# First loads, transposes and roundings in turns by K tile, squares later, constant products ahead of them, and operands at multiples of 512 bytes

## The chip, the core and the metric

The kernel runs on one core of a Trainium2 chip. A core has TensorE (PE), VectorE (DVE), ScalarE (ACT), GpSimd (POOL) and SyncE (SP, which here only issues DMAs). Each works through its own queue in order. The time is the device time of one execution in microseconds (us); lower is better.

## The reference

Two decoder layers over x, 256 tokens by 2048 features, float32:

```python
for l in range(DEPTH):                      # DEPTH = 2
    h = rmsnorm(x, attn_norm_g[l])
    q, k, v, gate_b, gate_c, conv_in = split(h @ w_in[l])      # 2048 x 6144
    attn = diff_attention(rmsnorm(q), rmsnorm(k), v, lam, rel_bias)   # 8 heads
    conv = gate_b * short_conv(gate_c * conv_in, conv_w[l])    # causal, 3 taps
    x = x + concat([rmsnorm(attn) * (1 - lam_init), conv]) @ w_out[l]
    x = x + relu(rmsnorm(x) @ w_up[l]) ** 2 @ w_down[l]        # 2048 x 8192 x 2048
```

All weights are float32 and are read once; the products with them are most of the work.

## The kernel before

Precision is kept by splitting every operand of a product into a rounded part (`hi`, type float32r) and the rest (`lo`). A product is then three TensorE instructions for each K tile of 128 rows: hi x hi, hi x lo, lo x hi (`TERMS`). The rounding is a copy on ACT (line 282 for weights, `whi`; line 248 for activations, `nT`), the rest a subtraction on DVE (line 283, `wlo`; line 249).

`linear` (line 325) makes 256 tokens by 512 columns out of 16 K tiles. Its weights come in jobs of two K tiles (512 KB, tile `raw`, four buffers). `Weights.take` hands out a job's halves and makes the halves of jobs up to three ahead (`AHEAD`). With `cut`, the first two jobs of the program are rounded one K tile at a time. After each K tile `linear` calls `work.tick()`: this advances the side work, a list of generators that each say after how many ticks they go on. So PE's order (which is the program's order) has transposes, norms and attention put between the products at fixed ticks. The order on the other engines is made by a planner, which takes its own estimate of when an operand is ready; `late` pins an instruction behind the one traced before it on its engine.

At the start of the program:

- x comes in four blocks of 512 columns, `load_x` (line 133). Block 0 is issued first, in two halves, then two weight jobs, block 1, two weight jobs, blocks 2 and 3, all on SP's queue.
- The norm's gains (`ngv`) are loaded from ACT's queue, transposed on PE (`gps`, line 152) and copied to `ngains`.
- `Norm.chunk(n)` transposes block n on PE (line 402, `tpn`, eight transposes into two PSUM banks), multiplies by the gains while it rounds (`split_gained`, lines 248 and 249), and at once takes the squares for the norm (line 412, `junk`). Block 0 goes first, the others at ticks of the first product.
- `Norm.factors` waits until all four blocks are transposed and makes the row scales; the norm itself is applied to the product's result, not to its operand. A broadcast of the scales (`rbc`, line 444) goes through PE.
- `qk_norm` (yield at line 474) normalises q and k after their products and transposes them eight ticks later.

The constants lie in a pool of their own at the lowest addresses (tiles are rounded up to 32 bytes per partition); pools of large tiles follow, and SBUF is full but for 160 bytes per partition.

Of the kernel before, what the change touches and what calls it, by code (L numbers as in the profile page):

```python
# [9 lines left out]
F32 = mybir.dt.float32  # L10
F32R = mybir.dt.float32r
AF = mybir.ActivationFunctionType
# [3 lines left out]
P = 128  # L16
DEPTH = 2
D = 2048
S = 256
NT = S // P  # L20
AW = 1024
NH = 8
# [6 lines left out]
CH = 512  # L29
WC = 256  # L30
KG = 4
RAW = 4
AHEAD = 3
# [68 lines left out]
def trunk(ctx: ExitStack, tc: tile.TileContext, x, w_in, w_out, conv_w, q_norm_g, k_norm_g,  # L102
          lambda_q1, lambda_k1, lambda_q2, lambda_k2, subln_g, attn_norm_g, mlp_norm_g,
          w_up, w_down, rel_bias, selector, out):
    nc = tc.nc
    PSUM = bass.MemoryType.PSUM
    const = ctx.enter_context(tc.tile_pool(name="const", bufs=1))
# [6 lines left out]
    mm = ctx.enter_context(tc.tile_pool(name="mm", bufs=2, space=PSUM))  # L114
    ps = ctx.enter_context(tc.tile_pool(name="ps", bufs=3, space=PSUM))
    ctx.enter_context(tc.manual_schedule(engines={mybir.EngineType.PE}))

    def late(ins):

        tc.keep_in_program_order(ins)  # L120

    def bank(name):
        return ps.tile([P, CH], F32, tag="bank", name=name)

    def wide(name):
        return nat.tile([P, CH], F32, tag="wide", name=name)

    work = Background()


    xs = [xpool.tile([P, NT, CH], F32, tag=f"x{n}", name=f"x{n}") for n in range(D // CH)]

    def load_x(n, cuts=1):
        for c in range(cuts):
            lo, hi = c * CH // cuts, (c + 1) * CH // cuts
            nc.sync.dma_start(
                xs[n][:, :, lo:hi],
                x[0, :, n * CH + lo:n * CH + hi].rearrange("(t p) c -> p t c", p=P))

    NG = DEPTH * D // P  # L140
    ngv = const.tile([NG, P], F32, tag="ngv", name="ngv")
    nc.scalar.dma_start(ngv, attn_norm_g.rearrange("l (k p) -> (l k) p", p=P))
    load_x(0, 2)

    ident = const.tile([P, P], F32, tag="ident", name="ident")
    make_identity(nc, ident)
    mhalf = const.tile([P, NH], F32, tag="mhalf", name="mhalf")
    nc.vector.memset(mhalf, -0.5)


    gps = bank("gps")
# [4 lines left out]
    def norm_gain(which, l, k):  # L156
        i = l * (D // P) + k
        return gains[:, MG + i:MG + i + 1] if which else ngains[:, i:i + 1]
# [19 lines left out]
    rel = const.tile([NB + 1, 2 * NH], F32, tag="rel", name="rel")  # L178
    nc.vector.memset(rel[NB:NB + 1, :], NEG)
    nc.gpsimd.dma_start(rel[0:NB, :], rel_bias)  # L180
    ones = const.tile([P, P], F32, tag="ones", name="ones")
    nc.vector.memset(ones, 1.0)

    gains = const.tile([P, ROWS], F32, tag="gains", name="gains")
    q_gain = const.tile([P, DEPTH], F32, tag="qg", name="q_gain")
    k_gain = gains[:, QG + DEPTH:QG + 2 * DEPTH]
# [59 lines left out]
    def split_gained(dst, k, src, gain):  # L246

        nc.scalar.activation(dst[:, 0, k], src, AF.Copy, scale=gain)  # L248
        nc.vector.scalar_tensor_tensor(
            dst[:, 1, k], src, gain, dst[:, 0, k].bitcast(F32), op0=ALU.mult, op1=ALU.subtract)  # L250
# [14 lines left out]
    class Weights:  # L265
# [5 lines left out]
            self.jobs, self.made, self.used = [], [], 0  # L271
            self.early = []

        def halves(self, raw, c=slice(None)):

            i = len(self.made)
            shape = [P] + list(raw.shape[1:])
            hi = wpool.tile(shape, F32R, tag="hi", name="whi")
            lo = wpool.tile(shape, F32R, tag="lo", name="wlo")
            first = self.cut and i < 2  # L280
            for k in (slice(0, 1), slice(1, None)) if first else (slice(None),):
                nc.scalar.activation(hi[:, k], raw[:, k], AF.Copy)  # L282
                nc.vector.tensor_sub(lo[:, k], raw[:, k], hi[:, k].bitcast(F32))  # L283
            return hi, lo

        cut = False

        def plain(self, w, row, c, nk):

            cols = 2 * CH // nk  # L290

            def make():
                raw = self.early.pop(0) if self.early else load()
                return self.halves(raw)

            def load():
                raw = self.pool.tile([P, nk, cols], F32, tag="raw", name="raw", bufs=RAW)
                nc.sync.dma_start(
                    raw, w[row:row + nk * P, c:c + cols].rearrange("(k p) c -> p k c", p=P))
                return raw  # L300

            make.load = load
            self.jobs.append(make)

        def load_early(self, n):

            for _ in range(n):
                self.early.append(self.jobs[len(self.early)].load())

        def take(self):  # L310
            i = self.used
            self.used += 1
            while len(self.made) < min(len(self.jobs), i + 1 + AHEAD):
                self.made.append(self.jobs[len(self.made)]())
            return self.made[i]

# [68 lines left out]
    class Norm:  # L385
# [2 lines left out]

        def __init__(self, which, l):
            self.which, self.l = which, l  # L390
            self.tiles = [Parts(apool, "a", f"nT{which}{l}_{n}") for n in range(D // CH)]
            self.ss = small.tile([P, NT, D // CH], F32, tag="ss", name=f"ss{which}{l}", bufs=2)

        def chunk(self, n, wait):
            yield wait
            a = self.tiles[n].open()
            for j in range(2):
                tp = bank(f"tpn{n}_{j}")
                for i in range(2):
                    k = 2 * j + i  # L400
                    for t in range(NT):
                        nc.tensor.transpose(  # L402
                            tp[:, i * S + t * P:i * S + (t + 1) * P],
                            xs[n][:, t, k * P:(k + 1) * P], ident)
                for i in range(2):
                    k = 2 * j + i
                    split_gained(a, k, tp[:, i * S:(i + 1) * S],
                                 norm_gain(self.which, self.l, n * KG + k))
            self.tiles[n].ready = True
            for t in range(NT):  # L410
                junk = wide(f"junk{n}_{t}")
                sq = nc.scalar.activation(junk, xs[n][:, t], AF.Square,
                                          accum_out=self.ss[:, t, n:n + 1])
                if (self.which, self.l) == (0, 0):
                    late(sq)

        def factors(self):
            while not all(t.ready for t in self.tiles):
                yield 1
            tot = small.tile([P, NT], F32, tag="tot", name="tot")  # L420
            nc.vector.tensor_reduce(tot, self.ss, axis=AX.X, op=ALU.add)
            r = rstd_of(tot, D, "row", NT)
            self.r = small.tile([P, NT], F32, tag="rowf", name="rowf", bufs=2)
            nc.vector.tensor_copy(self.r, r)
            diag = small.tile([P, NT, P], F32, tag="diag", name="diag", bufs=1)
            if self.which:

                self.scale = small.tile([P, 1], F32, tag="rowf2", name="rowf2")
                nc.vector.tensor_mul(self.scale, r[:, 1:2], r[:, 1:2])
                ratio = small.tile([P, 1], F32, tag="ratio", name="ratio")  # L430
                nc.vector.reciprocal(ratio, r[:, 1:2])
                nc.vector.tensor_mul(ratio, ratio, r[:, 0:1])
                nc.vector.tensor_scalar_mul(diag[:, 0], ident, ratio)
                yield 5
                tp = bank("rbc")
                nc.tensor.matmul(tp[:, :P], ones, diag[:, 0], start=True, stop=True)
                self.ratio = small.tile([P, P], F32, tag="rowb", name="ratiob", bufs=1)
                nc.vector.tensor_copy(self.ratio, tp[:, :P])
                return
            for t in range(NT):  # L440
                nc.vector.tensor_scalar_mul(diag[:, t], ident, self.r[:, t:t + 1])
            yield 5
            tp = bank("rbc")
            nc.tensor.matmul(tp[:, :S], ones, diag.rearrange("p t c -> p (t c)"),
                             start=True, stop=True)
            self.across = small.tile([P, 2, S], F32, tag="rowb", name="rowb", bufs=1)
            nc.vector.tensor_copy(self.across[:, 0], tp[:, :S])
            nc.gpsimd.tensor_tensor(self.across[:, 1], self.across[:, 0], self.across[:, 0],
                                    op=ALU.mult)
# [5 lines left out]
    def qk_norm(acc, r, dst, gain, name):  # L455

        out_ = []
        for t in range(NT):
# [6 lines left out]
            f = rstd_of(ms, DK, f"{name}{t}", NH)  # L465
# [5 lines left out]
                acc[:, t].rearrange("p (g d) -> p g d", d=DK),  # L471
                f2.unsqueeze(2).to_broadcast([P, NH, DK]), op=ALU.mult)
            out_.append(qn)
        yield 8
        for t in range(NT):
            tp = bank(f"{name}tp{t}")
            for i in range(4):
# [121 lines left out]
    def mixer(l, norm, loads):  # L599

        with ExitStack() as scope:
# [2 lines left out]
            rpool = scope.enter_context(tc.tile_pool(name="rpool", bufs=RAW))  # L604
            bpool = scope.enter_context(tc.tile_pool(name="bpool", bufs=8))
            weights = Weights(rpool)
            weights.cut = l == 0
            for half in range(2):
                for part in range(3):
                    weights.straight(w_in[l], 0, D // P, part * AW + half * CH)  # L610
# [373 lines left out]
    norm = Norm(0, 0)  # L984

    def first_loads(weights):
        for n in range(1, D // CH):
            weights.load_early(2)
            load_x(n)
            work.start(norm.chunk(n, 2), 4 * n - 3)  # L990

    work.start(norm.chunk(0, 0))
    for l in range(DEPTH):
        mnorm = mixer(l, norm, first_loads if l == 0 else lambda weights: None)
        norm = mlp(l, mnorm, l == DEPTH - 1)
# [31 lines left out]
```

## Time and profile before

| | |
|---|---|
| median of 3 runs | 2181.64 us (2178.86 to 2182.95) |
| the profiled execution | 2181.14 us |
| its span, first to last instruction | 2179.4 us |
| PE busy | 2156.6 us, 99% |
| DVE, ACT, POOL busy | 74%, 58%, 6% |
| DMA engines | 205 GB/s in the mean |

In the rows below a line of a group reads: line, engine, operation, out<-in, shape, xcount | busy us, mean ns of one | idle time before them and what ended it. A row of the timeline or of the chain begins with its start and its length in us. A row of a DMA issue ends with KB of one and the us from issue to landing. A row of a window gives its length, then each engine's busy us, the granted clock, the share of the DMA engines and GB/s.

### The profile page before, as it was taken

What the parts mean: (1) busy time and instruction counts of PE and PEld (TensorE: products, weight loads), DVE (VectorE), ACT (ScalarE), POOL (GpSimd) and SP (SyncE); (2) the same over time, 40 slices, a digit from 0 to 9 for tenths busy, and PEclk for the clock granted to TensorE, in tenths of its full rate; (3) what the DMA queues carried; (4) which work ended last, traced back from release to release, by engine and by line L of the source; (5) the groups of instructions that cost most, each with busy time, mean ns of one, the idle gap of its engine ahead of it and who ended that gap; (6) DMA issues with size and microseconds to landing.
All of it is one profiled execution on the core that took longest, in us unless ns stands there. A gap on an engine that the chain in (4) does not pass through costs nothing.

```text
span 2179.4 us, 29050 instructions
## 1 busy us (share of the span) xinstructions
PE 2156.6 (99%) x11066; PEld 1828.6 (84%) x11066; DVE 1603.9 (74%) x2229; ACT 1271.7 (58%) x1718; POOL 138.8 (6%) x194
## 2 busy tenths in 40 slices
PE   8999999999999999999999999999999999999999
PEld 6888888888888888888888888888888888888887
DVE  6677655698888888855566776557988888887554
ACT  6456445566666666654454654455666666665443
POOL 2021100000000000100011111000000000001000
PEclk9999999999999999999999999999999999999999
DMA  7555656476666666587565466656766666666774
GB/s 256 180 156 177 218 185 184 157 238 223 213 212 215 220 208 214 189 277 241 175 205 181 156 199 197 184 173 190 225 218 217 213 212 216 219 208 212 246 242 145
DMA packets 292491, 446.62 MB, mean 205 GB/s; under 512 B 10403, under 2 KB 191221, under 8 KB 292352
## 3 DMA queue, kind: packets, MB, share of 16 engines
q1 hardware_dynamic: 285648, 423.66, 61.5%
q0 software_dynamic: 6656, 21.10, 2.6%
q8 instruction: 86, 1.41, 0.3%
q14 instruction: 53, 0.43, 0.1%
q10 hardware_dynamic: 48, 0.02, 0.0%
HBM read 425.84 MB, written 18.90 MB: 204 GB/s over the span
## 4 chain that ended last, share of the span: by engine, by line
PE 94%; DMA 2%; DVE 2%; ACT 1%; issue 1%; SPq 0%; DVEq 0%; ACTq 0%
PE upc L809 29%; PE dn L969 15%; PE pr L849 13%; PE o L338 8%; PE q L338 4%; PE gc L360 4%; PE ci L360 4%; PE k L338 4%; PE gb L360 4%; PE v L338 4%; PE upw L809 1%; DMA uraw<-in_w_up_dram 1%; PE sc L500 1%; PE av L536 1%; PE tpn L402 1%; DMA draw<-in_w_down_dram 1%
## 5 line engine op out<-in xcount | busy, mean ns | idle before, releaser
L283 DVE TENSOR_TENSOR wlo<-raw,whi 128x1024 fp32r<-128x1024 f32 (+1 forms) x386 | 473.3, 1228 | 385.5 <-ACT whi L282 381.0
L282 ACT ACTIVATE whi<-raw 128x1024 fp32r<-128x1024 f32 (+1 forms) x386 | 406.8, 1055 | 477.8 <-PE dn L969 166.7
L809 PE MATMUL upc<-nT,uhi 128*128 128x512 f32 x1920 | 477.5, 391 | 0.0
L694 ACT ACTIVATE uhi<-uraw 128x1024 fp32r<-128x1024 f32 x256 | 271.2, 1060 | 287.3 <-PE upc L809 253.9
L809 PEld LDWEIGHTS upc<-nT,uhi 128*128 128x128 f32 x1920 | 352.7, 188 | 68.2
L695 DVE TENSOR_TENSOR ulo<-uraw,uhi 128x1024 fp32r<-128x1024 f32 x256 | 312.8, 1222 | 115.3 <-ACT uhi L694 112.9
L969 PE MATMUL dn<-whi,g 128*128 128x512 f32 x1024 | 316.4, 389 | 0.0
L809 PEld LDWEIGHTS upc<-nT,ulo 128*128 128x128 f32 x1920 | 261.9, 190 | 18.7
L809 PE MATMUL upc<-nT,ulo 128*128 128x256 f32 x1920 | 267.7, 282 | 0.0
L969 PEld LDWEIGHTS dn<-whi,g 128*128 128x128 f32 x1024 | 192.2, 188 | 39.7
L969 PE MATMUL dn<-wlo,g 128*128 128x512 f32 x512 | 199.6, 390 | 1.1 <-DVE wlo L283 1.0
L338 PE MATMUL o<-whi,cat 128*128 128x512 f32 x512 | 159.6, 390 | 0.0
L969 PEld LDWEIGHTS dn<-wlo,g 128*128 128x128 f32 x512 | 96.1, 188 | 22.6 <-DVE wlo L283 2.8
L338 PEld LDWEIGHTS o<-whi,cat 128*128 128x128 f32 x512 | 96.2, 188 | 19.7
L338 PE MATMUL o<-wlo,cat 128*128 128x512 f32 x256 | 99.6, 389 | 0.0
L831 POOL DMA_DIRECT2D hid<-h x64 | 34.9, 545 | 949.1 <-ACT h L830 913.4
L849 PE MATMUL pr<-t13h,f 128*128 128x512 f32 x240 | 93.8, 391 | 0.0
L338 PE MATMUL q<-whi,nT 128*128 128x512 f32 x256 | 86.4, 406 | 4.1 <-ACT nT L248 4.1
L338 PE MATMUL k<-whi,nT 128*128 128x512 f32 x256 | 85.3, 399 | 0.0
L849 PE MATMUL pr<-t24h,f 128*128 128x512 f32 x240 | 84.0, 391 | 0.0
L849 PE MATMUL pr<-b2h,f 128*128 128x512 f32 x240 | 84.0, 391 | 0.0
L338 PE MATMUL v<-whi,nT 128*128 128x512 f32 x256 | 83.4, 396 | 0.0
(330 smaller groups left out, 3431.0 us busy)
## 6 DMA issues: line engine op xcount, KB each, us to landing
uraw<-in_w_up_dram SPq DMA_DIRECT2D x128, 1024.0 KB, 5.9
raw<-in_w_in_dram SPq DMA_DIRECT2D x192, 512.0 KB, 3.9
draw<-in_w_down_dram SPq DMA_DIRECT2D x64, 1024.0 KB, 5.1
raw<-in_w_down_dram SPq DMA_DIRECT2D x64, 1024.0 KB, 5.7
raw<-in_w_out_dram SPq DMA_DIRECT2D x64, 512.0 KB, 3.6
hid<-h POOLq DMA_DIRECT2D x64, 256.0 KB, 4.3
back<-hid SPq DMA_DIRECT2D x32, 512.0 KB, 3.3
rev<-by_dist_d POOLq DMA_DIRECT2D x4, 1024.0 KB, 11.1
```

Source lines behind the costliest of these rows:

```text
L282: nc.scalar.activation(hi[:, k], raw[:, k], AF.Copy)
L283: nc.vector.tensor_sub(lo[:, k], raw[:, k], hi[:, k].bitcast(F32))
L338: nc.tensor.matmul(acc[:, t], a.ap[:, pa, k % KG, t * P:(t + 1) * P], (hi, lo)[pw][:, j], start=(k == 0 and n == 0), stop=(k == nk - 1 and ...
L360: nc.tensor.matmul(acc[:, f, 0] if part else acc[:, f], wt[:, k % 4, fs], a.ap[:, 0, k % KG] if part else a.ap[:, :, k % KG], start=(part ...
L402: nc.tensor.transpose(tp[:, i * S + t * P:i * S + (t + 1) * P], xs[n][:, t, k * P:(k + 1) * P], ident)
L500: nc.tensor.matmul(sc[:, :W], qT[m * DK:(m + 1) * DK, a, i, t * P:(t + 1) * P], kT[m * DK:(m + 1) * DK, b, i, :W], start=(n == 0), stop=(n ...
L694: nc.scalar.activation(hi, src, AF.Copy)
L695: nc.vector.tensor_sub(lo, src, hi.bitcast(F32))
L809: nc.tensor.matmul(acc[:, 0] if part else acc, wt[:, k], a.ap[:, 0, k % KG] if part else a.ap[:, :, k % KG], start=(part == 0 and kh == 0 ...
L831: nc.gpsimd.dma_start(hid[i // 2][:, i % 2 * 2 * S:(i % 2 + 1) * 2 * S], u)
L849: nc.tensor.matmul(prods[n], fs[j][:, pa, a], b[pw], start=(j == 0 and m == 0), stop=(stop and m == 2))
L969: nc.tensor.matmul(acc[:, t], f[:, pa, k, t * P:(t + 1) * P], (hi, lo)[pw][:, k % 2], start=(b == 0 and k == 0 and m == 0), stop=(b == NB2 ...
```

## The change

Five things change.

1. The first block of x and the first weight job are loaded in turns: half of the x block, the first K tile of weights, the other half, the second K tile. The other early loads keep their order.
2. `Norm.begin` transposes, rounds and splits block 0 one K tile at a time, and behind each K tile it rounds and splits the weights of that K tile (`part`). The instructions are pinned in this order.
3. The squares of blocks 0 to 2 come later: block 0's after all four K tiles, those of blocks 1 and 2 some ten ticks after their transposes. `factors` waits for the squares. The weights are made one job ahead at first, up to three ahead from the seventh job on (`ramp`).
4. `warm_up(n)` issues n products of a constant tile of ones (float32, 128 x 128 x 128) into a PSUM tile that nothing reads: 11 ahead of the first transpose, 3 after the second and 3 after the fourth K tile.
5. A tile `fill` of 128 bytes and a tile `started` are added to the constants, and `ngv` leaves them, so that the pools behind begin at a multiple of 512 bytes; they began 352 bytes past one.

`qk_norm` transposes 12 ticks later instead of 8.

```diff
+    const.tile([P, 32], F32, tag="fill", name="fill")
...
-    def load_x(n, cuts=1):
-        for c in range(cuts):
-            lo, hi = c * CH // cuts, (c + 1) * CH // cuts
-            nc.sync.dma_start(
+    def load_x(n, lo=0, hi=CH):
+        nc.sync.dma_start(
...
-    ngv = const.tile([NG, P], F32, tag="ngv", name="ngv")
+    ngv = wide("ngv")[:NG, :P]
     nc.scalar.dma_start(ngv, attn_norm_g.rearrange("l (k p) -> (l k) p", p=P))
-    load_x(0, 2)
+    ones = const.tile([P, P], F32, tag="ones", name="ones")
+    nc.vector.memset(ones, 1.0)
+    mhalf = const.tile([P, NH], F32, tag="mhalf", name="mhalf")
+    nc.vector.memset(mhalf, -0.5)
+    started = const.tile([P, 1], F32, tag="started", name="started")
+    nc.scalar.activation(started, mhalf[:, 0:1], AF.Copy)
+    warm = mm.tile([P, NT, CH], F32, tag="mm2", name="warm")
+
+    def warm_up(n):
+        for _ in range(n):
+            nc.tensor.matmul(warm[:, 0, :P], ones, ones, start=True, stop=True)
     ident = const.tile([P, P], F32, tag="ident", name="ident")
     make_identity(nc, ident)
+    warm_up(11)
...
         def halves(self, raw):
...
+            if not self.by_tile:
+                pair = (nc.scalar.activation(hi, raw, AF.Copy),
+                        nc.vector.tensor_sub(lo, raw, hi.bitcast(F32)))
+                if self.ramp and len(self.made) < 12:
+                    for ins in pair:
+                        late(ins)
             return hi, lo
...
+        def begin(self):
+            self.by_tile = self.ramp = True
+            raw = self.pool.tile([P, 2, CH], F32, tag="raw", name="raw", bufs=RAW)
+            w, row, c = self.first
+            for k in range(2):
+                load_x(0, k * CH // 2, (k + 1) * CH // 2)
+                nc.sync.dma_start(raw[:, k], w[row + k * P:row + (k + 1) * P, c:c + CH])
+            self.early.append(raw)
+            self.load_early(1)
+            raws = list(self.early)
+            self.made += [self.jobs[i]() for i in range(2)]
+            self.by_tile = False
+
+            def part(k):
+                (hi, lo), raw, j = self.made[k // 2], raws[k // 2], k % 2
+                late(nc.scalar.activation(hi[:, j], raw[:, j], AF.Copy))
+                late(nc.vector.tensor_sub(lo[:, j], raw[:, j], hi[:, j].bitcast(F32)))
+            return part
...
-            while len(self.made) < min(len(self.jobs), i + 1 + AHEAD):
+            ahead = min(AHEAD, max(1, i - 4)) if self.ramp else AHEAD
+            while len(self.made) < min(len(self.jobs), i + 1 + ahead):
...
             self.tiles[n].ready = True
+            if (self.which, self.l) == (0, 0) and n < D // CH - 1:
+                yield 12 - 2 * n
+            self.squares(n)
...
+        def begin(self, part):
+            a = self.tiles[0].open()
+            for k in range(KG):
+                tp = ps.tile([P, CH], F32, tag="av", name="tpb3", bufs=1) if k == KG - 1 else bank(f"tpb{k}")
+                for t in range(NT):
+                    nc.tensor.transpose(tp[:, t * P:(t + 1) * P],
+                                        xs[0][:, t, k * P:(k + 1) * P], ident)
+                if k % 2:
+                    warm_up(3)
+                split_gained(a, k, tp[:, :S], norm_gain(0, 0, k))
+                part(k)
+            self.tiles[0].ready = True
+            self.squares(0)
+            yield 1
...
         def factors(self):
-            while not all(t.ready for t in self.tiles):
+            while self.squared < D // CH:
                 yield 1
...
-        yield 8
+        yield 12
...
     def first_loads(weights):
+        part = weights.begin()
         for n in range(1, D // CH):
-            weights.load_early(2)
             load_x(n)
+            if n == 1:
+                weights.load_early(2)
             work.start(norm.chunk(n, 2), 4 * n - 3)
-
-    work.start(norm.chunk(0, 0))
+        work.start(norm.begin(part))
```

More of the change, by code (lines that the diff above doesn't have):

```diff
@@ L128, in trunk @@
     work = Background()
+    const.tile([P, 32], F32, tag="fill", name="fill")
     xs = [xpool.tile([P, NT, CH], F32, tag=f"x{n}", name=f"x{n}") for n in range(D // CH)]
-    def load_x(n, cuts=1):
-        for c in range(cuts):
-            lo, hi = c * CH // cuts, (c + 1) * CH // cuts
-            nc.sync.dma_start(
-                xs[n][:, :, lo:hi],
-                x[0, :, n * CH + lo:n * CH + hi].rearrange("(t p) c -> p t c", p=P))
+    def load_x(n, lo=0, hi=CH):
+        nc.sync.dma_start(
+            xs[n][:, :, lo:hi],
+            x[0, :, n * CH + lo:n * CH + hi].rearrange("(t p) c -> p t c", p=P))
     NG = DEPTH * D // P
-    ngv = const.tile([NG, P], F32, tag="ngv", name="ngv")
+    ngv = wide("ngv")[:NG, :P]
     nc.scalar.dma_start(ngv, attn_norm_g.rearrange("l (k p) -> (l k) p", p=P))
-    load_x(0, 2)
+    ones = const.tile([P, P], F32, tag="ones", name="ones")
[8 more added lines that the diff above has]
+            nc.tensor.matmul(warm[:, 0, :P], ones, ones, start=True, stop=True)
     ident = const.tile([P, P], F32, tag="ident", name="ident")
     make_identity(nc, ident)
-    mhalf = const.tile([P, NH], F32, tag="mhalf", name="mhalf")
-    nc.vector.memset(mhalf, -0.5)
+    warm_up(11)
     gps = bank("gps")
@@ L180, in trunk @@
     nc.gpsimd.dma_start(rel[0:NB, :], rel_bias)
-    ones = const.tile([P, P], F32, tag="ones", name="ones")
-    nc.vector.memset(ones, 1.0)
     gains = const.tile([P, ROWS], F32, tag="gains", name="gains")
@@ L272, in __init__, with halves @@
             self.early = []
-        def halves(self, raw, c=slice(None)):
-            i = len(self.made)
+        def halves(self, raw):
             shape = [P] + list(raw.shape[1:])
@@ L279, in halves @@
             lo = wpool.tile(shape, F32R, tag="lo", name="wlo")
[L280 to L283, printed above, removed]
-            return hi, lo
-        cut = False
+            if not self.by_tile:
[4 more added lines that the diff above has]
+                        late(ins)
+            return hi, lo
+        by_tile = ramp = False
+        def begin(self):
[15 more added lines that the diff above has]
+            return part
         def plain(self, w, row, c, nk):
@@ L302, in plain @@
             make.load = load
+            if not self.jobs:
+                self.first = w, row, c
             self.jobs.append(make)
@@ L307, in load_early @@
             for _ in range(n):
-                self.early.append(self.jobs[len(self.early)].load())
+                self.early.append(self.jobs[len(self.made) + len(self.early)].load())
         def take(self):
@@ L390, in __init__ @@
             self.which, self.l = which, l
+            self.squared = 0
             self.tiles = [Parts(apool, "a", f"nT{which}{l}_{n}") for n in range(D // CH)]
@@ L409, in chunk, with squares @@
             self.tiles[n].ready = True
+            if (self.which, self.l) == (0, 0) and n < D // CH - 1:
+                yield 12 - 2 * n
+            self.squares(n)
+        def squares(self, n):
+            self.squared += 1
             for t in range(NT):
@@ L606, in mixer @@
             weights = Weights(rpool)
-            weights.cut = l == 0
             for half in range(2):
```

## The prediction

> **What bounds the kernel now.** I read the page first, then the chain that ended last over the first 60 us, then the issues and landings of the first loads, then groups by shape on ACT and DVE.
>
> ```profile
> span 2179.4 us, 29050 instructions
> PE 2156.6 (99%) x11066; PEld 1828.6 (84%) x11066; DVE 1603.9 (74%) x2229; ACT 1271.7 (58%) x1718; POOL 138.8 (6%) x194
> PEclk9999999999999999999999999999999999999999
> PE 94%; DMA 2%; DVE 2%; ACT 1%; issue 1%; SPq 0%; DVEq 0%; ACTq 0%
> ```
>
> TensorE bounds everything: 99% busy, 94% of the chain. So the change can gain in three ways only: PE starts its products earlier, runs the first ones at a better pace, or runs all of them at a better pace. The chain at the start:
>
> ```profile
> 1.72 6.60 DMA raw<-in_w_in_dram
> 8.34 0.03 ACT whi L282
> ...
> 8.88 0.61 ACT whi L282
> 9.49 0.37 ACT nT L248
> ...
> 9.90 5.49 PE q L338 x12
> 15.39 1.15 PE tpn L402 x8
> 16.54 5.49 PE q L338 x24
> 22.03 0.87 PE tpn L402 x8
> ...
> 37.64 0.43 PE rbc L444 x2
> 39.47 10.89 PE k L338 x48
> ```
>
> Two losses stand here. The first product waits until 9.90: ACT takes the rounding of the first weights (`whi`, after the landing at 1.72 + 6.60 = 8.32) ahead of the rounding of the transposes (`nT`). And the first 12 products take 5.49 / 12 = 457 ns, the next 24 take 5.49 / 24 = 229 ns: half pace, though the page's granted clock reads full there. In the rest of the program the pace is even:
>
> ```profile
> 485.05 5.56 PE upc L809 x32
> 957.33 130.58 PE dn L969 x576
> ```
>
> 130.58 / 576 = 226.7 ns for 512 columns. Of the 32 in the first row half have 256 columns: 2 x 5.56 / 32 = 347.5 ns for a pair, so 120.8 ns for 256 columns. Doubling the columns adds 105.9 ns, so 14.9 ns of each are fixed.
>
> **The change part by part.** Times are measured against the profiled execution, 2181.14 us, of which 2179.4 are the span; it lies 0.5 us under the median of 2181.64. A difference of 0.2%, 4.4 us, is about what a measurement of this kernel can tell from none.
>
> *Loads in turns.* The first block of x is still loaded in two halves, and the first weights come now in two halves too, in turns with them: one more issue on SP.
>
> ```profile
> 1.72 0.98 SPq L298 DMA_DIRECT2D raw<-in_w_in_dram  x2
> ```
>
> An issue costs 0.49 us (0.98 / 2) and what follows on SP is issued that much later. The landings, from the DMA view of one issue each (issued at 1.21, 1.72, 2.23 and 2.74), with the load on the queues:
>
> ```profile
> x<-in_x_dram SPq DMA_DIRECT2D x1, 256.0 KB, 3.4
> raw<-in_w_in_dram SPq DMA_DIRECT2D x1, 512.0 KB, 6.6
> raw<-in_w_in_dram SPq DMA_DIRECT2D x1, 512.0 KB, 7.4
> x<-in_x_dram SPq DMA_DIRECT2D x1, 512.0 KB, 8.4
> 6.00:8.00 2.00, 0.00 (x0) 0.00 (x0) 0.00 (x0) 0.00 (x0) 0.88 (x2) 1.00 1.02 318
> ```
>
> They land in order, at 4.7, 8.3, 9.6 and 11.1, and the engines are full (share 1.02), so the later issue costs nothing. The order of bytes is the same after the first megabyte: the second K tile of weights still lands at about 8.3, the second weights at 9.6, the second block of x at 11.1. POOL's own issues stay as they are. The first K tile of weights is new: it takes the place of the second half of x, about 4.7; that half moves behind it, at 5.4 by the rate (256 KB at 318 GB/s), at 7.2 if it meets whatever holds back the tail of the 512 KB load.
>
> *Constant products.* 11 before the first transpose, 3 after each two K tiles; each is float32 and runs as two instructions, as `rbc` does.
>
> ```profile
> 1.04 0.17 DVE L182 MEMSET ones<- 128x128 f32 x1
> 3.50 0.31 PE L152 MATMUL gps<-ident,ngv 32*128 32x32 f32 x1 [3.50 <-POOL ident masks.py:199]
> 3.81 2.01 PE L402 MATMUL tpn<-ident,x 128*128 128x128 f32 x8
> ```
>
> `rbc`, with 256 columns, takes 0.43; with 128 columns 0.22, and 0.43 at half pace. The memset of `ones` (done at 1.21 now) moves to the front of DVE, so PE starts at about 1.1 and the 11 end at 1.1 + 11 x 0.43 = 5.8. The gains' transpose `gps` (0.31) waits in PE's order behind them: it moves from 3.5 to 5.8, the first transposes from 3.8 to 6.1. That cost of 2.3 us is covered only because ACT now waits for weights anyway. The pace rose within the transposes at 15.39, 5.5 to 6.0 us after dense work began at 9.90; from 1.1 that gives 6.6 to 7.1. So: four transposes at half pace (0.21 each, from 2.01 for 8) end at 6.95; three products at full pace (0.65) 7.6; four transposes (half of 0.87) 8.05; three products 8.7.
>
> The Trainium skill, "TensorE: Matmul & The Clock Gate" (Part 1), has the clock rise after one busy window of some 3.4 us that runs freely; as an estimate from that page it would rise between 4.5 and 7.9 here, and the products could start between 8.3 and 9.3. The trace's 5.5 to 6.0 us lies within one to two such windows.
>
> *Transposes and roundings in turns.* The rows that price them, ACT first, then DVE:
>
> ```profile
> L282 ACT ACTIVATE whi<-raw 128x1024 fp32r<-128x1024 f32 x9 | 9.5, 1055 | 6.9 <-PE q L338 3.5 <-issue 2.6 <-ACT whi L282 0.9
> L248 ACT ACTIVATE nT<-tpn,ngains 128x256 fp32r<-128x256 f32 x16 | 6.7, 466 | 2.9 <-DVE nT L249 2.9
> L412 ACT ACTIVATE junk<-x 128x512 f32<-128x512 f32 x8 | 5.0, 626 | 0.0
> L282 ACT ACTIVATE whi<-raw 128x512 fp32r<-128x512 f32 x4 | 2.3, 624 | 5.9 <-DMA raw<-in_w_in_dram 5.9
> ```
> ```profile
> L283 DVE TENSOR_TENSOR wlo<-raw,whi 128x1024 fp32r<-128x1024 f32 x8 | 9.8, 1222 | 5.5 <-ACT whi L282 5.3
> L249 DVE SCALAR_TENSOR_TENSOR nT<-tpn,ngains,nT 128x256 fp32r<-128x256 f32 x16 | 7.0, 477 | 0.3 <-ACT nT L248 0.2
> L283 DVE TENSOR_TENSOR wlo<-raw,whi 128x512 fp32r<-128x512 f32 x4 | 2.6, 686 | 5.0 <-ACT whi L282 5.0
> ```
>
> No instruction is added: four roundings of 128x512 and four `nT` were there already. ACT does `nT` of K tile 0 from 6.75 to 7.2, `whi` to 7.8; DVE ends `wlo` at 8.5. K tile 1 waits for its weights at 8.3: `whi` 8.95, `wlo` 9.6. So PE's own queue decides: products start at 8.8, 1.1 us earlier, and K tile 1, wanted at 8.8 + 6 x 0.227 = 10.2, is there. Tile 2 and 3 (weights at 9.6) are done by 10.9 and 12.0.
>
> The half pace goes: 5.49 - 12 x 0.229 = 2.74, and 1.15 - 0.87 = 0.28 in the transposes: 3.0 us.
>
> *What is late next.* The ramp makes weights only one job ahead for six jobs. A job feeds 12 products, 2.72 us. With a block of transposes in between, ACT has 1.06 + 4 x 0.42 = 2.7 us of work and DVE 1.22 + 4 x 0.44 = 3.0, against 2.72 + 0.87 = 3.6 on PE: it fits, with little to spare. I take 0.5 us of new waits; the bounds are 0 and 9 us (below).
>
> *Squares put off.* Eight as before, 0.63 us each, at later ticks; the row scale comes after the last and `rbc` (0.43 of PE either way) moves into the next product. Who waits is the q norm, whose accumulator the third product needs 23 us later: nothing.
>
> *q and k transposes four ticks later* (12 instead of 8; a tick is 6 x 0.227 = 1.36 us).
>
> ```profile
> 73.10 0.44 PE k00tp L478 x4
> ...
> 88.97 0.49 PE sc L500 x6
> ```
>
> The attention scores use them at 88.97. Moved by 5.4 us the k transposes end near 80.8, and ACT and DVE need some 2 us: 6 us of cover are left. Cost nothing; without the cover, 2 us at each of four places.
>
> *One `started` copy on ACT* runs ahead of any landing: nothing. The load of the gains lands in another tile: nothing.
>
> *Alignment.* The constants of the kernel before end 352 bytes past a multiple of 512, and every pool behind them holds multiples of 512, so all large operands share that remainder. The change takes 512 bytes away and adds 32 + 128: remainder 0. No row shows an aligned 512-column operand. Upper bound on PE: the fixed cost of all 11066 instructions, 14.9 ns each, 165 us. Lower: nothing; a loss isn't likely, since all operands share one remainder before and after. I take nothing for the pace. The other place is landings. All of PE's waits outside the start:
>
> ```profile
> PE up L809 <- ACT ev L819: 3.2, 2, 2.0
> PE pr L849 <- DVE f L841: 3.2, 4, 1.0
> PE pr L935 <- DVE wlo L283: 1.6, 2, 0.8
> PE rbc L436 <- DVE diag L433: 1.1, 2, 0.5
> PE dn L969 <- DVE wlo L283: 1.0, 2, 0.6
> ```
> ```profile
> 410.72 1.06 ACT L694 ACTIVATE uhi<-uraw 128x1024 fp32r<-128x1024 f32 x1 [3.22 <-DMA uraw<-in_w_up_dram]
> ```
>
> 10.1 us in all; the first row, 3.2 us at the entry of the two MLPs, hangs on a landing (ACT waited 3.22 us for `uraw`). Bounds: 0 to 10 us; I take half of 3.2, 1.6.
>
> The Trainium skill, "DMA: Bandwidth & Descriptors" (How a descriptor splits into AXI transactions), counts transactions of 256 bytes from aligned addresses, so a 2 KB run that begins 96 past one would need 9 instead of 8. The same page (Specifications) puts a core's share of memory at about 358 GB/s, near the 318 of the row above; by that limit alignment would give nothing back, and the sum would be 2177.5.
>
> *Sum:* -1.1 (start) - 3.0 (pace) + 0.5 (new waits) - 1.6 (landings) = -5.2: 2181.14 - 5.2 = 2175.9, rounded 2176.
>
> **The rivals.** *Only the start counts* (chance 0.16): alignment changes nothing and the new waits are 1 to 2 us. For it: the queues are full in the first microseconds whatever the addresses. Then 2181.1 - 4.1 + 1 = 2178, within 0.2%.
>
> *The constant products don't lift the pace* (0.10): the clock isn't raised by them, or falls again between them. Against it: they are as dense as the products at 9.90. Then the second three end at 10.6 instead of 8.7, the 12 products still cost 457 ns, and 0.7 us are lost: 2182.
>
> *Slower: conversions come just in time and miss* (0.10). Place: ACT and DVE between the second and the eighth weight job. It decides as soon as the time from taking a job to the end of its `wlo` passes 2.72 us; one rounding after the other needs 1.06 + 1.22 = 2.28, and four `nT` queued ahead on ACT add 1.7. If the six ramped jobs are each late by 1.5 us, 9 us are lost against 4.1 won: 2186. Against it: the `nT` fall into three of the eight jobs only.
>
> *The pace of all products falls with alignment* (0.10): 2176 - 165 = 2011, if the 14.9 ns go whole. For it: they are the same for 512 and 256 columns, as a cost per operand would be. Against it: nothing shows that they hang on the address.
>
> **How the numbers follow.** The forecast has 0.54: 2166 (all 10 us of waits gone) to 2177.3. Faster by over 0.2%: 0.54 + 0.10 = 0.64. Within: 0.16 + 0.10 = 0.26. Slower: 0.10. The range leaves out the pace case and the slower one: 2166 to 2183; the likeliest's own is 2166 to 2177.3.
>
> **What would show it.** First product of q at 8.8 +- 0.5 with the next 11 at 227 ns; `k` beginning at about 35 instead of 39.47; the 576 `dn` products still at 226.7 ns; the MLP's first wait at 410 shorter. A first product after 10, products at 427 ns, or waits of `q` for `wlo` would make the start wrong; a changed pace in `dn` would make the whole wrong.

## The result, and the profile after

The changed kernel takes 2186.38 us (median of 13 runs, 2183.82 to 2187.84) against 2181.69 of the kernel before in the runs beside it: a ratio of 1.0024, 95% interval 1.0016 to 1.0032. It is 4.7 us slower where 5.2 us faster was forecast.

The head of the page, changed kernel:

```profile
span 2184.6 us, 29117 instructions
...
PE 2162.1 (99%) x11100; PEld 1834.5 (84%) x11100; DVE 1605.8 (74%) x2229; ACT 1271.7 (58%) x1719; POOL 135.3 (6%) x194
```

Nothing here tells of the loss. Three views of the first 70 us do. The chain that ended last there (start, length, what):

```profile
9.13 4.13 PE q L373 x18
...
32.80 2.81 PE q L373 x11
35.61 0.02 issue
...
36.72 1.23 DVE wlo L290
37.95 0.17 DVE tot L479
...
39.24 0.18 DVE rowf L482
...
39.45 0.70 ACT q00sq L519
...
40.17 0.70 DVE q00ms L521
...
44.24 0.70 ACT q00sq L519
...
48.57 1.23 DVE wlo L290
...
49.84 10.61 PE k L373 x35
...
66.83 3.17 PE v L373 x14
```

The start is as forecast: q begins at 9.13 with products of 4.13 / 18 = 229 ns. q ends at 35.6 and k begins, 3.9 us earlier than the 39.47 of before. Then the chain leaves PE for 14.2 us (35.61 to 49.84): it runs through the weight job taken just before (`wlo`), the row scale (`tot`, `rowf`), the whole q norm of both row tiles, and only then a `wlo`. By the start of v the 3.9 us are lost and more; the same point in the chain of before:

```profile
62.21 10.89 PE v L338 x48
```

v begins at 66.83 instead of 62.21, 4.6 us later, nearly the whole difference in the medians (4.7). What PE waited for between 30 and 70 us in the changed kernel (us in total, times, longest):

```profile
PE k L373 <- DVE wlo L290: 3.4, 1, 3.4
PE k L373 <- ACT whi L289: 1.7, 1, 1.7
```

Before, PE waits for nothing there. Two rows of windows, 35 to 68 us (length, then busy us of PE, PEld, DVE, ACT, POOL, the granted clock, DMA share, GB/s), before:

```profile
35.00:68.00 33.00, 33.00 (x151) 27.28 (x150) 21.42 (x29) 19.34 (x26) 6.88 (x9) 1.00 0.73 240
```

and after:

```profile
35.00:68.00 33.00, 27.89 (x115) 22.36 (x114) 16.64 (x23) 17.30 (x26) 5.18 (x7) 0.90 0.54 187
```

PE stands for 33.00 - 27.89 = 5.1 us, and the granted clock is 0.90 in the mean: after the second wait, the products run at half pace for a while. The 35 that the chain has from 49.84 on take 10.61 us, 2.7 more than 35 x 0.227 = 7.9; so the two waits cost some 7.8 us in all. ACT's order shows what stood in the way (changed kernel, timeline of ACT; in brackets the idle time before and what ended it):

```profile
36.60 0.61 ACT L454 ACTIVATE junk<-x 128x512 f32<-128x512 f32 x1
...
39.45 0.69 ACT L519 ACTIVATE q00sq<-q,rowf 128x512 f32<-128x512 f32 x1 [1.53 <-DVE rowf L482]
44.24 0.69 ACT L519 ACTIVATE q00sq<-q,rowf 128x512 f32<-128x512 f32 x1 [4.10 <-DVE q00n L527]
44.83 1.05 ACT L289 ACTIVATE whi<-raw 128x1024 fp32r<-128x1024 f32 x1
```

ACT sits idle for 4.10 us between the two squares of the q norm, and the rounding that k waits for (`whi`) comes behind the second. On DVE, by the chain, the `wlo` at 48.57 comes behind the whole norm in the same way.

### The profile page after: what moved, and what is told of

It reads as the page before. It is cut to its first block, busy times and chain, and to the rows that moved or that the text cites. A ratio compares the mean times of both kernels' runs of the same rounds, so it can differ in the third digit from the quotient of the medians.

```text
span 2184.6 us, 29117 instructions
## 1 busy us (share of the span) xinstructions
PE 2162.1 (99%) x11100; PEld 1834.5 (84%) x11100; DVE 1605.8 (74%) x2229; ACT 1271.7 (58%) x1719; POOL 135.3 (6%) x194
## 4 chain that ended last, share of the span: by engine, by line
PE 93%; DVE 3%; DMA 2%; ACT 1%; issue 1%; POOL 0%; DVEq 0%; ACTq 0%
PE upc L866 28%; PE dn L1026 15%; PE pr L906 12%; PE o L373 8%; PE ci L395 4%; PE gc L395 4%; PE gb L395 4%; PE v L373 4%; PE q L373 4%; PE k L373 4%; PE upw L866 1%; DMA uraw<-in_w_up_dram 1%; DMA draw<-in_w_down_dram 1%; PE sc L558 1%; PE av L594 1%
## 5 line engine op out<-in xcount | busy, mean ns | idle before, releaser
L290 DVE TENSOR_TENSOR wlo<-raw,whi 128x1024 fp32r<-128x1024 f32 x382 | 471.6, 1236 | 379.3 <-ACT whi L289 378.2
L289 ACT ACTIVATE whi<-raw 128x1024 fp32r<-128x1024 f32 x382 | 404.3, 1059 | 470.3 <-PE dn L1026 168.1
```

Of the source, the lines that this page charges most:

```text
L289: pair = (nc.scalar.activation(hi, raw, AF.Copy), nc.vector.tensor_sub(lo, raw, hi.bitcast(F32)))
L290: nc.vector.tensor_sub(lo, raw, hi.bitcast(F32)))
```

## The experiments

*Theory 1*: `late` is the cause. It pins the twelfth weight job (the fourth of k), the last one for which `len(self.made) < 12` holds. That job is taken when k begins, when the q norm is already traced, so on ACT and on DVE its `whi` and `wlo` stand behind the whole q norm. *Theory 2*: the late row scale by itself is the cause, since the squares are put off. *Theory 3*, in the first texts: the new addresses cost time.

**The pin.** The same kernel, the pin ended one job earlier:

```diff
-                if self.ramp and len(self.made) < 12:
+                if self.ramp and len(self.made) < 11:
```

> The changed kernel with one number changed: the first 11 weight jobs are pinned in program order instead of the first 12. Theory 1 (the pin of the twelfth job puts its rounding on ACT and its subtraction on DVE behind the q norm, which waits for the row scale and for POOL): the two stalls in the k product (1.9 and 3.7 us) and the half pace behind them go, 7 us or so, about 2179. Theory 2 (the row scale itself comes too late, because the squares do): the stalls stay, 2186. Theory 3 (the new addresses cost): 2186.

2177.95 us (11 runs; ratio to before 0.9987, 0.9978 to 0.9996). The order on ACT in this kernel:

```profile
39.83 1.06 ACT L289 ACTIVATE whi<-raw 128x1024 fp32r<-128x1024 f32 x1 [2.49 <-DMA raw<-in_w_in_dram]
...
41.84 0.67 ACT L519 ACTIVATE q00sq<-q,rowf 128x512 f32<-128x512 f32 x1
42.41 1.05 ACT L289 ACTIVATE whi<-raw 128x1024 fp32r<-128x1024 f32 x1
```

The planner, left free, puts the `whi` ahead of the q norm and others between its steps. PE waits for nothing in k, and in the chain of this kernel v begins 8.6 us earlier than in the changed one:

```profile
35.02 5.44 PE k L373 x24
...
58.21 16.33 PE v L373 x72
```

One comparison changed by one is worth 8.4 us (2186.38 - 2177.95), and the kernel is then faster than the kernel before, too (2180.65 beside it). By the ratios, which take out what the kernel before moved between the two sets of runs, it is 0.0037, 8.1 us. The same kernel again, as the base for others:

> The changed kernel with the pin ending one job earlier, once more, as the base for the runs beside it. If the first measurement holds, 2177.5 against 2180.2 of the kernel before (ratio 0.9987); its chain begins k near 35 and v near 58 in every profile where the first half of x lands by 6.

2178.47 us against 2179.39 of before beside it, ratio 0.9991 (0.9982 to 1.0000). So the kernel is some 1 to 3 us faster than before, and the pin costs 7 to 8 us.

Does the pin need the other edits? The kernel before, with this pin alone (line 282 and 283; `i` is the job's index):

```diff
-                nc.scalar.activation(hi[:, k], raw[:, k], AF.Copy)
-                nc.vector.tensor_sub(lo[:, k], raw[:, k], hi[:, k].bitcast(F32))
+                pair = (nc.scalar.activation(hi[:, k], raw[:, k], AF.Copy),
+                        nc.vector.tensor_sub(lo[:, k], raw[:, k], hi[:, k].bitcast(F32)))
+                if self.cut and i == 11:
+                    for ins in pair:
+                        late(ins)
```

> The kernel before, in which one thing is changed: the rounding and the subtraction of the twelfth weight job are pinned behind what was traced before them, as the changed kernel does. Theory 1 (the pin holds them behind the chain of the q norm, and that is the whole loss): k waits for wlo some 5 to 6 us and a few products behind the wait run at half pace, 5 to 9 us in all, so 2186 to 2190 against 2181. Theory 3 (the pin needs the other edits, the late squares or the short ramp, to hurt): within 1.5 us of before.

2183.80 us, ratio 1.0015 (1.0006 to 1.0024): 3.6 us slower than before (2180.20 beside it). Theory 3 of this text (the pin needs the other edits; not the addresses) falls: the pin hurts alone. Theory 1's sign holds, at a smaller size than it gave, and the other edits double the price. PE's wait and the chain of this kernel:

```profile
PE k L341 <- DVE wlo L283: 3.3, 1, 3.3
```
```profile
1.73 5.09 DMA raw<-in_w_in_dram
...
8.41 5.42 PE q L341 x12
...
36.21 1.41 PE q L341 x6
37.62 0.03 ACTq L282
...
40.01 0.61 DVE q00ms L466
...
48.05 1.23 DVE wlo L283
...
49.32 2.84 PE k L341 x11
```

The lengths of the two chains go with the two sizes. Three jobs of k are ready when it begins: 3 x 2.72 = 8.2 us of cover. Here the chain from the end of q to the pinned `wlo` is 49.32 - 37.62 = 11.7 us, 3.5 more than the cover, and PE waits 3.3. In the changed kernel it is 14.2 us against 8.2 + 0.43 (`rbc` falls into k now), 5.6 more, and PE stands for 5.1. Of the 2.5 us by which the chain is longer, 2.2 lie ahead of the first `q00ms` (40.17 - 35.61 = 4.6 against 40.01 - 37.62 = 2.4): there the row scale is now made, behind the end of q (`tot` at 37.95, `rowf` at 39.24), as the last squares come late (`junk`, 36.60). The rest of the difference is the pace behind the wait: here the 11 products take 2.84 us, 0.3 more than at full pace, so wait and pace cost 3.6 us against 7.8 in the changed kernel. This is one execution, the fastest of the 11 (2180.46); that the pace holds in the others too isn't shown.

**The squares.** The changed kernel with the squares of blocks 1 and 2 at once behind their transposes:

```diff
-            if (self.which, self.l) == (0, 0) and n < D // CH - 1:
-                yield 12 - 2 * n
             self.squares(n)
```

> The changed kernel with the squares of blocks 1 and 2 taken right behind their transposes again; the pin stays on 12 jobs. Theory 1: the q norm starts some 3 us earlier but the twelfth job still stands behind it; a stall of 1 to 2 us is left, about 2180 to 2181. Theory 2: all of the stall goes, 2179. Theory 3: 2186.

2187.03 us, ratio 1.0027 (1.0017 to 1.0038). Theory 2 falls: with an early row scale the kernel is no faster. Theory 1's own number was missed too, by 6 us, because the squares cost something elsewhere. PE's waits in this kernel, 0 to 70 us:

```profile
PE k L373 <- DVE wlo L290: 3.0, 1, 3.0
PE q L373 <- DVE wlo L290: 2.8, 2, 2.1
```

k's wait is shorter than in the changed kernel (3.0 against 5.1), but q has waits that the changed kernel has not. Both edits together:

> Pin ending one job earlier, and the squares of blocks 1 and 2 at once behind their transposes again. From the waits of the run with the squares alone (0.86 and 2.36 us in q, which the changed kernel does not have) the put-off squares are worth about 3 us: 2181. If they are worth nothing once the pin is gone, 2178.

2182.79 us, ratio 1.0010 (1.0001 to 1.0018): 4.8 us above the 2177.95 of the kernel with the squares put off, more than the 3 expected. k waits for nothing, q still does:

```profile
PE q L373 <- DVE s_gain L219: 2.0, 1, 2.0
...
PE q L373 <- DVE wlo L290: 0.8, 1, 0.8
```

So the two edits bear on each other (ratios to before):

| | squares put off | squares at once |
|---|---|---|
| twelfth job pinned | 1.0024 (the change) | 1.0027 |
| pin ends before it | 0.9987, 0.9991 | 1.0010 |

Putting the squares off gains 4 to 5 us (0.0019 to 0.0023) where the pin doesn't reach the twelfth job, and nothing that can be told where it does: by then it makes the chain longer that the pin puts ahead of k. The pin costs 3.7 us (0.0017) with the squares at once, 7 to 8 with them put off.

**Twelve ticks.** The kernel without the harmful pin, q and k transposed after 8 ticks again:

```diff
-        yield 12
+        yield 8
```

> As the base, but q and k are transposed 8 ticks after their norms again instead of 12. The prediction costs this edit at nothing: within 1 us of the base. If the late row scale makes the transposes of q wait for q00n (its last ends near 48, and 8 ticks after the start of the third product's work is near 46), PE waits some 2 us and runs several products at half pace: 2180 to 2182.

2185.68 us, ratio 1.0029 (1.0019 to 1.0039), 7.2 us more than its base (2178.47). PE's waits:

```profile
PE q00tp L536 <- DVE q00n L527: 5.0, 2, 3.7
```

The wait is the one expected, and it is longer. With the late row scale the q norm isn't done after 8 ticks, and the four more are enough: with them PE doesn't wait for it. (No run has 8 ticks with the squares at once and the shorter pin, so that it is the late scale that needs them is read from the order, not tested.)

**The constant products.** The base without any of them:

```diff
-        for _ in range(n):
+        for _ in range(0):
             nc.tensor.matmul(warm[:, 0, :P], ones, ones, start=True, stop=True)
```

> The changed kernel with the pin ending one job earlier (2178.0) and without the constant products. If they are worth what the rows of before say (2.7 us of half pace in the first 12 products and 0.3 in the transposes), the time is 3 us longer, 2181; q's first products take about 427 ns until some 5 to 6 us after the first transpose. If the pace rises by itself, or the start is then bound by ACT and DVE and not by PE, it is within 1 us of 2178.

2177.78 us, ratio 0.9986 (0.9977 to 0.9994), against 2177.95 with them. Its chain:

```profile
7.23 6.30 PE q L373 x18
13.53 0.87 PE tpn L438 x8
```

q begins 1.9 us earlier than at 9.13, since nothing stands ahead of the transposes or between them; its first 18 products take 6.30 instead of 4.13 us, 2.2 more. So the 18 end at 13.53, against 9.13 + 4.13 = 13.26 in the changed kernel: the constant products win 0.3 us there. The changed kernel's is the latest start of the nine profiled kernels that have all 17 products: the transposes behind the 18 begin at 11.76 to 13.10 in them and at 13.37 here, so the win is 0.3 to 1.6 us at this place, against a single execution without them (in which k later waits 0.4 us for a `wlo`). In the medians no gain shows, and none of 3 us.

With the 11 ahead, and none between the transposes:

```diff
                 if k % 2:
-                    warm_up(3)
+                    warm_up(0)
```

> As the base, but with the 11 constant products ahead of the transposes alone, without the three and three between them. By the run without any, the transposes themselves aren't delayed by the 11 (first transpose at 6.34 against 6.14), and the three and three put the first product of q off by 1.3 us (6 x 0.22). If the pace stays up without them, the first product comes at 7.4 and the time is 1.3 us shorter, 2176.2; if it falls back between the transposes, q's first 12 products take up to 2.7 us more: 2179.

2179.05 us, ratio 0.9998 (0.9989 to 1.0006), against 2178.47 of its base: no difference shown. The first products of q in this kernel's timeline of PE say why:

```profile
7.83 0.49 PE L373 MATMUL q<-whi,nT 128*128 128x512 f32 x1 [0.43 <-ACT whi L315]
8.56 0.50 PE L373 MATMUL q<-wlo,nT 128*128 128x512 f32 x1 [0.23 <-DVE wlo L316]
```

PE comes sooner and then waits for the first K tile's rounding: the six between the transposes lie in time that PE would wait anyway.

**The addresses.** The kernel before with a fill of 160 bytes and `ngv` in another pool, so that its operands begin at multiples of 512:

```diff
+    const.tile([P, 40], F32, tag="fill", name="fill")
...
-    ngv = const.tile([NG, P], F32, tag="ngv", name="ngv")
+    ngv = wide("ngv")[:NG, :P]
```

> The kernel before with its constants made up to a multiple of 512 bytes (160 bytes added, the gains' tile moved out of them), nothing else. Theories 1 and 2: nothing changes at the products, 2181.7; if landings profit, 2180. Theory 3 (the addresses cost): 2185 or more. The prediction's rival of a faster pace: far below 2150.

2178.30 us, ratio 0.9988 (0.9979 to 0.9996). The changed kernel 352 bytes past a multiple again, and the kernel with the shorter pin likewise:

```diff
-    const.tile([P, 32], F32, tag="fill", name="fill")
+    const.tile([P, 120], F32, tag="fill", name="fill")
```

> The changed kernel with its large operands back at 352 bytes past a multiple of 512. Theories 1 and 2: as the changed kernel, 2186. Theory 3: 2181 or less.

> Pin ending one job earlier, operands 352 bytes past a multiple of 512 again as in the kernel before. If the remainder matters for landings (the kernel before gained 2.3 us when its operands were put at multiples), 2180; if that gain was the order of the first landings alone, which the loads in turns now set, 2178.

2185.79 us (1.0022, 1.0013 to 1.0030) against 2186.38, and 2179.47 (0.9994, 0.9986 to 1.0003) against 2177.95: the signs differ, the intervals overlap, and neither expectation of the last run can be told from the other. The 576 products of `dn`, first in the changed kernel, then with 352 bytes:

```profile
962.17 130.59 PE dn L1026 x576
```
```profile
962.04 130.59 PE dn L1026 x576
```

226.7 ns in both, as before. That the kernel before gained 2.4 us by its fill (2178.30 against 2180.65) stays unexplained: the pace can't be it. In its profile q begins at 8.19 instead of 9.90, but at the old addresses, in the kernel with the pin alone, it begins at 8.41. This gain also takes something from the change: the kernel with the shorter pin (0.9987, 0.9991) isn't faster than the kernel before with the fill (0.9988), and at the old addresses its 0.9994 can't be told from 1. So a gain in time from the loads in turns, apart from the addresses, isn't shown.

**The other pins.** The base with no weight job behind the first two pinned:

```diff
-                if self.ramp and len(self.made) < 11:
+                if self.ramp and len(self.made) < 0:
```

> As the base, but none of the weight jobs behind the first two is pinned. If only the twelfth job's pin does harm and the others nothing, within 1 us of the base; if the other pins keep nT ahead of the roundings where it matters, a wait of q for nT or wlo shows, and 1 to 3 us more.

2180.60 us, ratio 1.0002 (0.9993 to 1.0011), against 2178.47. A wait of q for the transposes' roundings appears:

```profile
PE q L373 <- DVE nT L258: 0.7, 2, 0.6
```

So the pins of the third to the eleventh job seem to be worth some 2 us; the intervals overlap, so this is likely and not settled.

## Why the prediction was wrong

- **The step that failed** is "Squares put off ... Who waits is the q norm, whose accumulator the third product needs 23 us later: nothing." The q norm does have that time. But it isn't alone in its queues: by the new pin, the twelfth weight job stands behind it on ACT and DVE, and k needs that job 8.6 us after q ends. The diff shows that pin (`late(ins)` under `len(self.made) < 12`); the sum gave it no term. It costs 7 to 8 us here and 3.6 in the kernel before; the late row scale, which lengthens the chain by 2.2 us, and the half pace behind the wait make most of the difference. And the term itself isn't nothing: where the pin ends earlier, putting the squares off gains 4 to 5 us.
- **The ramp** ("it fits, with little to spare", 0.5 us) was right for the stretch that it was worked out for: no wait of q for its weights in the changed kernel. The working stopped at the eighth job; the wait came at the twelfth.
- **The slower rival** had the time (2186) and the kind of loss, weights that come too late, but not the place: not ACT and DVE being too busy (ACT idles 4.10 us at the crucial point), but the order of two in-order queues. Its sum, six jobs late by 1.5 us each, didn't happen; that the time fits is luck.
- **Start and pace** (-1.1 and -3.0): k "at about 35" came at 35.6, 3.9 us earlier, so the forecast of that moment was nearly right. But not all of the 3.9 us is gain. 0.43 is `rbc`, which now lies in k. And part of it lies in the profiled execution of the kernel before: in it the first weights landed at 8.32, in the kernel before with the pin alone at 6.82 (1.73 + 5.09) with the same issues, and k began at 37.62 instead of 39.47. That leaves 1.6 to 3.4 us, and the kernel with the shorter pin, where all of it should show, measures 1 to 3. The shares aren't borne out: the text gave 3.0 to the pace, which the constant products were to lift, but the kernel without them is no slower. In the pair shown above they gain 2.2 us of pace and put q off by 1.9, so by these traces most of the earlier k comes from the loads and roundings in turns. (In passing, the sum takes 0.21 us for a transpose at half pace from a row that gives 2.01 / 8 = 0.25; the four took 1.02.)
- **Landings in the rest of the program** (-1.6): the row that the term hung on went from 3.2 to 2.9 us, 0.3 and not half. Over all the kernels here it lies between 2.2 and 3.4 us with the operands at multiples of 512, and between 2.5 and 3.4 without, so no share of the addresses shows.

```profile
PE up L866 <- ACT ev L876: 2.9, 2, 1.5
```

- **The pace of all products**: rightly taken as unchanged.
- **The transposes four ticks later**: "Cost nothing" was right of the edit: no wait of PE in the changed kernel hangs on these transposes. The text asked what they delay and not what they allow: with 8 ticks, the kernel with the late squares and the shorter pin takes 7.2 us more.

## What to carry to other kernels

An instruction pinned "behind all that is traced so far" takes its place from the moment of tracing: ask for the last instruction that a pin covers what was traced just before it on each engine, and compare the chain of that with the cover (here 14.2 us against 8.6). When work is put off, go through its followers and through all that is queued behind those followers; idle time of an engine in the middle of a chain, as ACT's 4.10 us, can be the sign of such an order. And a first landing taken from one profile may be off by 1.5 us, so a start term of 1 us needs a second execution before it is believed.

## What the runs showed of the hardware

The moment at which the pace of the products rises isn't tied to the work. The 22 instructions of the first constant products, alike in all kernels that have them, first in the changed kernel and then in the one with 352 bytes:

```profile
1.04 5.06 PE L156 MATMUL warm<-ones 128*128 128x128 f32 x22 [1.04 <-DVE mhalf L148]
...
6.27 1.09 PE L465 MATMUL tpb<-ident,x 128*128 128x128 f32 x4
```
```profile
1.04 4.07 PE L156 MATMUL warm<-ones 128*128 128x128 f32 x22 [1.04 <-DVE mhalf L148]
...
5.21 0.66 PE L465 MATMUL tpb<-ident,x 128*128 128x128 f32 x4
```

In the one all 22 run at half pace and the first four transposes as well (1.09 us against 0.66), so the rise comes near 7; in the other a part of the 22 is already fast, so it comes before 5.1. With the same instructions from the same 1.04 us, it moves by some 2 us or more from one execution to the next. The Trainium skill, "TensorE: Matmul & The Clock Gate" (Part 1), has a window of about 3.4 us that runs freely and isn't set back by the start of the work; the spread measured here fits into such a window, and it is wider than the 500 ns either way that the same section gives. The prediction's single 5.5 to 6.0 us, read off one execution, is one draw from it.

After PE's two waits in k (1.7 and 3.4 us, one product between them), ten products took 54.27 - 49.84 = 4.4 us, half pace again:

```profile
49.84 0.80 PE L373 MATMUL k<-wlo,nT 128*128 128x512 f32 x1 [3.42 <-DVE wlo L290]
...
54.27 0.96 PE L373 MATMUL k<-whi,nT 128*128 128x512 f32 x2
```

Here the waits cost 2 to 3 us beyond themselves. It isn't so each time: in the kernel before with the pin, the 11 products behind a wait of 3.3 us took 2.84 us (258 ns each), nearly full pace.
